# Splits of weights ordered behind copies of partial sums, and a shifted rotation of PSUM banks, in a two-layer decoder trunk

## The chip, the core and the metric

The kernel runs on one core of a Trainium2 chip. A core has five engines that work side by side, each through its own queue of instructions: PE (TensorE: matmuls, which write to the accumulator memory PSUM), DVE (VectorE), ACT (ScalarE), POOL (GpSimd) and SP (SyncE, which here only starts transfers). The metric is the device time of one execution in microseconds (us), lower is better; the median of several runs is given.

## The reference

The input is one sequence of 512 tokens with 1024 features. Two layers are run, each of three sub-layers that are added to `x`: half of a SwiGLU feed-forward (hidden width 2816), a mixer, half of a second feed-forward.

```python
def swiglu(h, w_gate, w_up, w_down):
    return (jax.nn.silu(h @ w_gate) * (h @ w_up)) @ w_down
...
    for l in range(DEPTH):
        x = x + 0.5 * swiglu(rms_norm(x, ffn1_norm[l]), ffn1_w_gate[l], ffn1_w_up[l], ffn1_w_down[l])
        h = rms_norm(x, mix_norm[l])
        a, g, q, k, v = jnp.split(h @ w_in[l], splits, axis=-1)
        conv_out = conv_module(a, g, conv_w[l], conv_b[l], conv_norm[l])
...
        x = x + jnp.concatenate([conv_out, diff_out], axis=-1) @ w_out[l]
        x = x + 0.5 * swiglu(rms_norm(x, ffn2_norm[l]), ffn2_w_gate[l], ffn2_w_up[l], ffn2_w_down[l])
```

`conv_module` is a gated causal depthwise convolution of 31 taps; `diff_out` is a differential attention with four heads (two softmax maps each, biased by distance). All is float32.

## The kernel before

**Exact products from parts.** A float32 operand is split into a high part (rounded to the matmul's own type) and a low part (the rest), and a product is made of three matmuls: high by high, high by low, low by high. `parts_of` (L98 on) splits a weight tile: ACT copies it to `whi` (L100), DVE, or POOL in the mixer, subtracts to get `wlo` (L101). The tiles come from rings: five slots for raw weights (`wraw`), four for sums of weights (`wsum`), nine each for `whi` and `wlo`. A split can run when its raw tile is there and a slot of the rings is free.

**The feed-forward.** The 22 hidden blocks of 128 are done in three parts: "first" (6 blocks, plain products), "seven" (8) and "last" (8). In the last two, products of two by two blocks are made with seven block products instead of eight. Gate and up weights of a hidden block make one *group*: from the four halves `g1`, `g2`, `u1`, `u2` (loaded by SP, and by POOL where a transfer adds to what is in the tile, L159) come the seven operands `u2u1`, `u2`, `g1`, `g2`, `all`, `g1u2u1`, `g1u1` (class `Sums`; `all` and `g1u2u1` are added on DVE, L174 and L175). `seven` (L390 on) runs a group: four accumulators `a`, `d` (one PSUM bank) and `b`, `c` (the other), 256 columns each; each `go` adds 12 matmuls (L407) to one of them. Between them ACT saves partial sums in `keep` (L412, L416, L421), because the accumulators go on to add the next product. The last product of a group (`rest`, with `g1u1`) runs inside the next group, through `before`. `Hidden.add` (L445 on) then splits the hidden block (ACT L456, DVE L457) and, at every second one, makes the sums of blocks (DVE L462 to L464, ACT L466, DVE L467); `big`, `sum` and `last` are handles to these.

**The down products** of a part run as four *pairs* of output blocks (`Pair`, L477 on, matmuls L496) in the same scheme, with their own groups of weights. `head` makes the first product into `c` and saves it (L503). For pair 0 `body` makes `a`, saves it (L513), makes most of `b` and `d`, runs the head of pair 1, then the rest, and saves `a` and `d` (L523). For the others it makes `d`, runs the finish of the pair before, makes `a`, saves both (L529), makes `b`, `c`, `a`, and saves `a` (L533).

**Banks.** `pair_banks` (L345) gives two PSUM banks of one of three tags, which rotate: sc, po, mm. Each tag has two banks, so a tag comes round at every third request. In the mixer fixed tags meet this rotation: `softmaxes` uses sc and po, `project_values` uses mm, the output projection sc and po. The mixer asks in this order: two pairs in `begin` for the convolution, one for `conv_in(2)`, two for the keys, two for the queries, one for `conv_in(3)`. `to_features` transposes queries (PE L818) in the bank of their product, and ACT copies them out (L825).

**What sets the order.** The program is traced as text; when it is built, a scheduler puts each engine's instructions in an order with the help of a simulated timeline, among instructions that are ready there, and adds the semaphores. Matmuls marked `keep_in_program_order` stay in the order of the text. `behind(i, ...)` adds to each instruction that is traced inside it and runs on the engine of `i` an edge that puts it after `i`; it is an order on that engine alone, so with a handle of ACT it holds the high parts (L100), with one of DVE the low parts (L101).

In the function `ffn`, `fetch` starts the loads of a group's sums, `group` the rest, and `weights` or `split` the splits. Only two places were ordered by `behind` in the pairs: the splits made for pair 0 behind `hid.big` and `hid.sum`, those of pair 1 behind `hid.last`.

Of the kernel before, what the change touches and what calls it, by code (L numbers as in the profile page):

```python
# [22 lines left out]
KT = DM // P  # L23
# [46 lines left out]
def trunk(ctx: ExitStack, tc: tile.TileContext, xt, par, lamv, relb, onehot,  # L70
# [271 lines left out]

    turns = iter(range(1000))

    def pair_banks():  # L345
        tag = ("sc", "po", "mm")[next(turns) % 3]
        return [bank(tag, "ps_pair") for _ in range(2)]


    class Halves:  # L350
# [32 lines left out]
        def get(self, name):  # L383
# [3 lines left out]
            k0, c = {"b11": (0, 0), "t1": (0, HS), "b21": (KT // 2, 0), "b22": (KT // 2, HS)}[name]  # L387
            return lambda j: (acth[:, k0 + j, c : c + HS], actl[:, k0 + j, c : c + HS])

    def seven(halves, w, banks, fp, before, last):  # L390

        a, d = banks[0][:, :HS], banks[0][:, HS:]
        b, c = banks[1][:, :HS], banks[1][:, HS:]
        two = banks[1].rearrange("p (n c) -> p n c", n=2)
        keep = fp.tile([P, 4, HS], F32, tag="gn", name="keep", bufs=2)
        g = keep[:, 0::2]

        def go(ps, wt, xt, first=False):  # L400


            at = halves.get(xt)
            for j in range(KT // 2):
                (wh, wl), (xh, xl) = wpart([w[wt]], j), at(j)
                for i, (l, r) in enumerate(((wh, xh), (wh, xl), (wl, xh))):
                    mm = T.matmul(ps, l, r, start=first and i == j == 0, stop=False, skip_group_check=True)  # L407
# [69 lines left out]
    class Pair:  # L477
# [25 lines left out]
            self.saved = S.activation(self.keep[:, self.kc], self.c, AF.Copy)  # L503
            return self

        def body(self, w, before):
            a, b, c, d, go = self.a, self.b, self.c, self.d, self.go
            both = self.banks[0].rearrange("p (n c) -> p n c", n=2)
            if self.m == 0:
                n = self.hid.n  # L510
                most, rest = range(n - 1), range(n - 1, n)
                go(a, w["g1"], "b11")
                S.activation(self.keep[:, 0], a, AF.Copy)  # L513
# [9 lines left out]
                S.activation(self.keep[:, 2:], both, AF.Copy)  # L523
            else:
                nxt = None
                go(d, w["u2"], "t4")
                before()
                go(a, w["g1"], "b11")
                S.activation(self.keep[:, :2], both, AF.Copy)  # L529
                go(b, w["g2"], "b21")  # L530
                go(c, w["all"], "b22")
                go(a, w["g1u2u1"], "t2")
                S.activation(self.keep[:, 2], a, AF.Copy)  # L533
# [17 lines left out]
    def ffn(fp, pr, gu, dn, after, begun, then, aside=None):  # L551
        halves = None
        late = []
        jobs = []
# [20 lines left out]
        for fs, kind in PARTS:  # L575
            many = len(fs)
            hh, held = [], []
            if kind == "first":
# [55 lines left out]
            pair = None  # L634
            for m in range(KT // 2):
                m2 = m + KT // 2
                if m == 0:
                    with behind(hid.big, hid.sum):
                        ahead[0].split("u2u1")
                        this.split("all", "g1u2u1", "g1u1")  # L640
                    pair = Pair(hid, fp, m, m2).head(this.w["u2u1"])
                    nxt = pair.body(this.w, lambda: Pair(hid, fp, 1, 1 + KT // 2).head(ahead[0].w["u2u1"]))
                else:
                    if m == 1:
                        with behind(*hid.last):
                            this = group()
                            this.weights()
                        pair = nxt
                    else:
                        this = group()  # L650
                        this.weights()
                        pair = Pair(hid, fp, m, m2).head(this.w["u2u1"])
                    pair.body(this.w, finish)
                if kind == "last":
                    if m:
# [366 lines left out]
    for l in range(DEPTH):  # L1022
# [12 lines left out]
        with tc.tile_pool(name="ffn", bufs=1) as fp:  # L1035
            begun = ffn(fp, pr, gu1[l], dn1[l], preparing("mix_norm"), begun,
                        lambda tail: begin(nxt["p"], [[wag[l, c, i] for i in range(2)] for c in range(2)], tail),
                        aside if l == 0 else None)
        mixer(l, nxt["p"], preparing("ffn2_norm"), begun)
        with tc.tile_pool(name="ffn", bufs=1) as fp:  # L1040
            begun = begin(nxt["p"], [[gu2[l, m, i] for i in range(2)] for m in range(2)])
            if l + 1 < DEPTH:
                begun = ffn(fp, nxt["p"], gu2[l], dn2[l], preparing("ffn1_norm", l + 1), begun,
                            lambda tail: begin(nxt["p"], [[gu1[l + 1, m, i] for i in range(2)] for m in range(2)], tail))
            else:
                ffn(fp, nxt["p"], gu2[l], dn2[l], store, begun, lambda tail: tail())
        pr = nxt["p"]


# [72 lines left out]
```

## Time and profile before

| | us |
|---|---|
| median of three runs | 1803.24 (1803.14 to 1806.4) |
| the profiled execution | 1801.71 |
| its span, first to last instruction | 1799.7 |
| granted TensorE clock, mean over the span | 0.997 |

| stretch of PE (start to end in the profiled execution) | from | to |
|---|---|---|
| first feed-forward of layer 0, up groups of "seven" | 108.4 | 189.2 |
| its pairs | 189.1 | 229.7 |
| up groups of "last" | 229.5 | 311.8 |
| its pairs | 311.6 | 353.6 |
| output projection of the mixer of layer 0 | 508.5 | 555.3 |
| output projection of the mixer of layer 1 | 1400.9 | 1450.0 |

In a group's row stand the engine, the line, the operation and the tiles written and read; then the number of instructions, their busy time, the mean duration of one in ns, and the idle time of the engine before them with what ended it. A row of waits reads: who waited, for whom, total us, times, longest. A row of the order in time reads: start, duration, engine, line, operation, tiles, shapes, and in brackets the idle time before it and what ended it. Times are from the start of the span. Rows of several alike instructions in a run are merged (x2, x8).

### The profile page before, as it was taken

The page shows a single profiled execution, that of the slowest core. Times are in us where ns is not written, and L with a number is a line of the kernel's source. Part 1 is how long each engine was busy: PE and PEld are TensorE (multiplying, and loading weights), DVE is VectorE, ACT ScalarE, POOL GpSimd, SP SyncE. Part 2 cuts the span into 40 slices and gives each one's busy share as a digit, 9 for nine tenths or more (in the row PEclk, how much of TensorE's full clock was granted, in tenths as well). Part 3 has the DMA queues.
Part 4 walks back from the last instruction along what each step waited for, and adds up shares of the span by engine and source line. Part 5 has one row for each costly group of instructions (what it writes and reads, how often), then busy time and mean ns, then how long its engine had stood idle before and what let it go on. Part 6 is the DMA issues. An engine that isn't in the chain of part 4 may idle for free.

```text
span 1799.7 us, 33063 instructions
## 1 busy us (share of the span) xinstructions
PE 1768.5 (98%) x11844; PEld 1622.7 (90%) x11844; DVE 1477.8 (82%) x2595; ACT 1034.1 (57%) x1930; POOL 554.6 (31%) x523
## 2 busy tenths in 40 slices
PE   8999999999999999999999999999999999999998
PEld 7799999988778899999988999999877888999998
DVE  7969888969867869889977788888688588698886
ACT  5546566655845446566644565666558454465664
POOL 3011212379942011112310111133897320112121
PEclk9999999999999999999999999999999999999999
DMA  6457777633212547777643677766231135577774
GB/s 219 133 139 184 176 185 173 153 101 105 60 48 88 140 119 181 170 190 177 152 126 108 154 185 177 184 160 168 78 99 48 48 106 132 127 186 176 180 179 123
DMA packets 163012, 253.57 MB, mean 141 GB/s; under 512 B 18871, under 2 KB 60614, under 8 KB 162848
## 3 DMA queue, kind: packets, MB, share of 16 engines
q1 hardware_dynamic: 126144, 197.19, 35.4%
q0 software_dynamic: 36416, 54.12, 18.8%
q8 instruction: 92, 1.51, 0.4%
q14 instruction: 72, 0.59, 0.1%
q10 hardware_dynamic: 288, 0.16, 0.0%
HBM read 249.28 MB, written 3.42 MB: 140 GB/s over the span
## 4 chain that ended last, share of the span: by engine, by line
PE 90%; ACT 4%; DVE 2%; issue 1%; DMA 1%; POOL 1%; SPq 0%; ACTq 0%; DVEq 0%; POOLq 0%
PE ps_pair L407 36%; PE ps_pair L496 14%; PE ps_pair L202 9%; PE ps_pair L199 9%; PE ps_pair L203 9%; PE ps_out L199 2%; PE ps_out L202 2%; PE ps_out L203 2%; PE ps_pair L781 2%; PE ps_pair L780 2%; PE ps_pair L779 2%; ACT whi L100 1%; PE ps_sc L896 1%; DVE wlo L101 1%; PE ps_v L809 1%
## 5 line engine op out<-in xcount | busy, mean ns | idle before, releaser
L100 ACT ACTIVATE whi<-wraw 128x512 fp32r<-128x512 f32 x736 | 448.8, 628 | 465.4 <-PE ps_pair L202 160.1
L101 DVE TENSOR_TENSOR wlo<-wraw,whi 128x512 fp32r<-128x512 f32 x648 | 445.1, 709 | 113.5 <-ACT whi L100 98.1
L159 POOL DMA_DIRECT2D wsum<-in_gu x128 | 112.2, 912 | 717.4 <-DMA wsum<-in_gu 302.0
L407 PE MATMUL ps_pair<-actl,whi 128*128 128x256 f32 x1024 | 290.2, 283 | 0.0
L407 PE MATMUL ps_pair<-acth,wlo 128*128 128x256 f32 x1024 | 290.2, 283 | 0.0
L407 PE MATMUL ps_pair<-acth,whi 128*128 128x256 f32 x1024 | 290.2, 283 | 0.0
L407 PE MATMUL ps_pair<-tl,whi 128*128 128x256 f32 x768 | 217.7, 283 | 0.0
L407 PE MATMUL ps_pair<-th,wlo 128*128 128x256 f32 x768 | 217.7, 283 | 0.0
L407 PE MATMUL ps_pair<-th,whi 128*128 128x256 f32 x768 | 217.7, 283 | 0.0
L199 PE MATMUL ps_pair<-acth,whi 128*128 128x512 f32 x512 | 200.8, 395 | 5.6 <-ACT whi L100 5.6
L202 PE MATMUL ps_pair<-actl,whi 128*128 128x512 f32 x512 | 200.2, 392 | 0.0
L203 PE MATMUL ps_pair<-acth,wlo 128*128 128x512 f32 x512 | 199.1, 391 | 0.0
L407 PEld LDWEIGHTS ps_pair<-acth,whi 128*128 128x128 f32 x1024 | 196.8, 192 | 0.2
L407 PEld LDWEIGHTS ps_pair<-actl,whi 128*128 128x128 f32 x1024 | 196.8, 192 | 0.2
L407 PEld LDWEIGHTS ps_pair<-acth,wlo 128*128 128x128 f32 x1024 | 196.8, 192 | 0.0
L159 POOL DMA_DIRECT2D wsum<-in_dn x112 | 99.0, 1191 | 266.0 <-DVE wlo L101 108.0
L101 DVE TENSOR_TENSOR wlo<-wsum,whi 128x512 fp32r<-128x512 f32 x192 | 131.7, 693 | 30.6 <-ACT whi L100 29.3
L407 PEld LDWEIGHTS ps_pair<-th,whi 128*128 128x128 f32 x768 | 147.6, 192 | 0.0
L407 PEld LDWEIGHTS ps_pair<-th,wlo 128*128 128x128 f32 x768 | 147.6, 192 | 0.0
L407 PEld LDWEIGHTS ps_pair<-tl,whi 128*128 128x128 f32 x768 | 147.6, 192 | 0.0
L100 ACT ACTIVATE whi<-wsum 128x512 fp32r<-128x512 f32 x192 | 118.8, 623 | 47.1 <-PE ps_pair L202 16.7
L496 PE MATMUL ps_pair<-hl,whi 128*128 128x256 f32 x512 | 145.1, 283 | 0.0
(201 smaller groups left out, 4498.7 us busy)
## 6 DMA issues: line engine op xcount, KB each, us to landing
wraw<-in_gu SPq DMA_DIRECT2D x288, 256.0 KB, 3.5
wsum<-in_gu SPq DMA_DIRECT2D x128, 256.0 KB, 3.8
wsum<-in_gu POOLq DMA_DIRECT2D x128, 256.0 KB, 4.9
wraw<-in_dn SPq DMA_DIRECT2D x68, 256.0 KB, 3.5
wraw<-in_wqkv SPq DMA_DIRECT2D x48, 256.0 KB, 2.8
wraw<-in_dn SPq DMA_DIRECT2D x64, 128.0 KB, 4.0
wraw<-in_wag SPq DMA_DIRECT2D x32, 256.0 KB, 3.0
wraw<-in_wout SPq DMA_DIRECT2D x32, 256.0 KB, 2.9
```

The lines of the kernel that those rows point to most:

```text
L100: S.activation(hi, raw, AF.Copy)
L101: (eng or V).tensor_tensor(out=lo, in0=raw, in1=f32(hi), op=ALU.subtract)
L159: nc.gpsimd.dma_start(dst[:, to], src, accum_op=ALU.add)
L199: first = T.matmul(ps, wh, xh, start=start, stop=False)
L202: T.matmul(ps, wh, xl, start=False, stop=False)
L203: T.matmul(ps, wl, xh, start=False, stop=stop)
L407: mm = T.matmul(ps, l, r, start=first and i == j == 0, stop=False, skip_group_check=True)
L496: mm = T.matmul(ps, s[:, f], r, start=side not in self.begun, stop=False, skip_group_check=True)
L779: T.matmul(ps[n], xh[:, t], wh, start=k == 0, stop=False)
L780: T.matmul(ps[n], xh[:, t], wl, start=False, stop=False)
L781: T.matmul(ps[n], xl[:, t], wh, start=False, stop=k == KT - 1)
L809: T.matmul(ps, xh[:, t], wh, start=k == 0, stop=False)
```

## The change

First, the splits of a group are traced inside `group` and stand behind a copy: `saves` collects the copies that end a group's or a pair's use of `keep` (L421, L523, L533), and a group's splits come behind the last but one of them at that point of the text, or behind what `after` names (for pair 1 `hid.last`, as before). For pair 0 the splits of `all`, `g1u2u1` and `g1u1` move out of the block behind `hid.big` and `hid.sum`: they are now traced inside `body`, behind the copy L513 and behind `hid.last[0]` (L466). Second, `skip` passes over turns of the bank rotation: in the first feed-forward of layer 0 one turn before the down products of "first" and one before the groups of "seven"; in its second feed-forward and in the first of layer 1 one before "seven"; none in the last.

```diff
+    def skip(n):
+        for _ in range(n):
+            next(turns)
...
+    saves = []
...
-        S.activation(keep[:, 2], a, AF.Copy)
+        saves.append(S.activation(keep[:, 2], a, AF.Copy))
...
-        def body(self, w, before):
+        def body(self, w, before, more=None):
...
-                S.activation(self.keep[:, 0], a, AF.Copy)
+                more(S.activation(self.keep[:, 0], a, AF.Copy))
...
-                S.activation(self.keep[:, 2:], both, AF.Copy)
+                saves.append(S.activation(self.keep[:, 2:], both, AF.Copy))
...
-                S.activation(self.keep[:, 2], a, AF.Copy)
+                saves.append(S.activation(self.keep[:, 2], a, AF.Copy))
...
-        def group():
-            ahead[0].loads()
+        def group(part=False, after=()):
+            this = ahead[0]
+            this.loads()
             fetch()
-            return ahead.pop(0)
+            ahead.pop(0)
+            with behind(*(after or saves[-2:-1])):
+                if part:
+                    this.split("u2u1", "g1", "g2")
+                    this.add()
+                    this.split("u2")
+                else:
+                    this.weights()
+            return this
...
+                skip(spare[0])
...
+            if kind == "seven":
+                skip(spare[1])
             for mm, m in enumerate(fs):
-                rest = seven(halves, group().weights(), pair_banks(), fp, finish, mm == many - 1)
+                rest = seven(halves, group().w, pair_banks(), fp, finish, mm == many - 1)
...
-            this = group()
-            this.split("u2u1", "g1", "g2")
-            this.add()
-            this.split("u2")
+            this = group(part=True)
...
                 if m == 0:
+
+                    def more(saved):
+                        with behind(saved, hid.last[0]):
+                            this.split("all", "g1u2u1", "g1u1")
+
                     with behind(hid.big, hid.sum):
                         ahead[0].split("u2u1")
-                        this.split("all", "g1u2u1", "g1u1")
                     pair = Pair(hid, fp, m, m2).head(this.w["u2u1"])
...
-                    if m == 1:
-                        with behind(*hid.last):
-                            this = group()
-                            this.weights()
-                        pair = nxt
-                    else:
-                        this = group()
-                        this.weights()
-                        pair = Pair(hid, fp, m, m2).head(this.w["u2u1"])
+                    this = group(after=hid.last if m == 1 else ())
+                    pair = nxt if m == 1 else Pair(hid, fp, m, m2).head(this.w["u2u1"])
```

More of the change, by code (lines that the diff above doesn't have):

```diff
@@ L549, in begin, with ffn @@
         return [*zip(ws, ps)], first_products(pr, ws, ps, early=tail is not None, tail=tail)
-    def ffn(fp, pr, gu, dn, after, begun, then, aside=None):
+    def ffn(fp, pr, gu, dn, after, begun, then, spare, aside=None):
         halves = None
@@ L637, in ffn @@
                 if m == 0:
+                    def more(saved):
+                        with behind(saved, hid.last[0]):
+                            this.split("all", "g1u2u1", "g1u1")
                     with behind(hid.big, hid.sum):
                         ahead[0].split("u2u1")
-                        this.split("all", "g1u2u1", "g1u1")
                     pair = Pair(hid, fp, m, m2).head(this.w["u2u1"])
-                    nxt = pair.body(this.w, lambda: Pair(hid, fp, 1, 1 + KT // 2).head(ahead[0].w["u2u1"]))
+                    nxt = pair.body(this.w, lambda: Pair(hid, fp, 1, 1 + KT // 2).head(ahead[0].w["u2u1"]), more)
                 else:
-                    if m == 1:
-                        with behind(*hid.last):
-                            this = group()
-                            this.weights()
-                        pair = nxt
-                    else:
-                        this = group()
-                        this.weights()
-                        pair = Pair(hid, fp, m, m2).head(this.w["u2u1"])
+                    this = group(after=hid.last if m == 1 else ())
+                    pair = nxt if m == 1 else Pair(hid, fp, m, m2).head(this.w["u2u1"])
                     pair.body(this.w, finish)
@@ L1037, in trunk @@
                         lambda tail: begin(nxt["p"], [[wag[l, c, i] for i in range(2)] for c in range(2)], tail),
-                        aside if l == 0 else None)
+                        (l == 0, 1), aside if l == 0 else None)
         mixer(l, nxt["p"], preparing("ffn2_norm"), begun)
@@ L1043, in trunk @@
                 begun = ffn(fp, nxt["p"], gu2[l], dn2[l], preparing("ffn1_norm", l + 1), begun,
-                            lambda tail: begin(nxt["p"], [[gu1[l + 1, m, i] for i in range(2)] for m in range(2)], tail))
+                            lambda tail: begin(nxt["p"], [[gu1[l + 1, m, i] for i in range(2)] for m in range(2)], tail), (0, 1))
             else:
-                ffn(fp, nxt["p"], gu2[l], dn2[l], store, begun, lambda tail: tail())
+                ffn(fp, nxt["p"], gu2[l], dn2[l], store, begun, lambda tail: tail(), (0, 0))
         pr = nxt["p"]
```

## The prediction

> **What bounds the kernel now.** I read the page first, then TensorE's waits, then the order of work on each engine around the longest of them.
>
> ```profile
> PE 1768.5 (98%) x11844; PEld 1622.7 (90%) x11844; DVE 1477.8 (82%) x2595; ACT 1034.1 (57%) x1930; POOL 554.6 (31%) x523
> L407 PE MATMUL ps_pair<-actl,whi 128*128 128x256 f32 x1024 | 290.2, 283 | 0.0
> PE ps_pair L496 <- ACT keep L513: 6.8, 8, 0.8
> PE ps_pair L496 <- ACT keep L533: 3.1, 4, 1.2
> PE ps_pair L496 <- ACT keep L523: 1.7, 8, 0.2
> PE ps_out L199 <- ACT acth L880: 1.4, 2, 1.2
> PE ps_v L809 <- DVE gl L751: 0.8, 1, 0.8
> ```
>
> PE sets the end: it is busy for 98% of the span, and the up-product groups (L407) never wait. What can be won lies in a few waits. Eight equal ones (two in each feed-forward: one per part) end with the copy L513, eight with L523, four with L533; the rest shown is in the mixers. So 11.6 us (6.8 + 3.1 + 1.7) are waits of PE for copies on ACT. The first of the eight L513 waits:
>
> ```profile
> 192.78 0.28 PE L496 MATMUL ps_pair<-hl,whi 128*128 128x256 f32 x1
> 192.90 0.28 PE L496 MATMUL ps_pair<-hh,wlo 128*128 128x256 f32 x1
> 194.02 0.39 PE L496 MATMUL ps_pair<-yh,whi 128*128 128x256 f32 x1 [0.84 <-ACT keep L513]
> 194.25 0.28 PE L496 MATMUL ps_pair<-yl,whi 128*128 128x256 f32 x1
> 190.70 0.38 ACT L503 ACTIVATE keep<-ps_pair 128x256 f32<-128x256 f32 x1 [1.48 <-PE ps_pair L496]
> 191.53 0.61 ACT L100 ACTIVATE whi<-wsum 128x512 fp32r<-128x512 f32 x1
> 192.05 1.14 ACT L100 ACTIVATE whi<-wraw 128x512 fp32r<-128x512 f32 x2
> 193.09 0.61 ACT L100 ACTIVATE whi<-wsum 128x512 fp32r<-128x512 f32 x1
> 193.61 0.36 ACT L513 ACTIVATE keep<-ps_pair 128x256 f32<-128x256 f32 x1
> 193.88 0.83 ACT L466 ACTIVATE yh<-ht 128x768 fp32r<-128x768 f32 x1
> ```
>
> PE computes `a` (12 matmuls), nine of `b`, then wants `d`, which shares `a`'s bank and so waits until L513 has read `a`. Matmuls follow each other at 0.12 us here, so `a` is complete nine matmuls and one drain before 192.90 + 0.12: its last starts at 191.82 and ends at 192.10. The copy runs only at 193.61, because ACT, which had no idle time between, is making four high parts: one for the next pair, then `all`, `g1u2u1`, `g1u1` of this one.
>
> **Part 1: three splits go behind L513 and L466.** New order on ACT: 191.53 the next pair's high part, L513 at 192.14 (its `a` is there), done 192.50; `d` may start at 193.02 without a wait. The gap goes from 1.12 us start to start to 0.12, and the slow second start (194.02 to 194.25, 0.23) goes too: 1.11 us, times 8 = **8.9 us**. What is late next is `all`:
>
> ```profile
> 191.79 0.42 DVE L464 SCALAR_TENSOR_TENSOR ht<-ht,hid 128x256 f32<-128x256 f32 x1
> 192.73 0.68 DVE L101 TENSOR_TENSOR wlo<-wsum,whi 128x512 fp32r<-128x512 f32 x1
> 195.14 0.95 DVE L467 TENSOR_TENSOR yl<-ht,yh 128x768 fp32r<-128x768 f32 x1
> 198.53 0.69 DVE L175 TENSOR_TENSOR wraw<-wraw 128x512 f32<-128x512 f32 x1
> ```
>
> L466 needs L464 (done at 192.21), so it follows L513: 192.50 to 193.33; the high part of `all` is there at 193.9. DVE does the next pair's low part until 193.4, L467 until 194.35, the low part of `all` until 195.0. PE does nine of `d` (1.08) and the next pair's head (1.44), wants `all` at 195.54 and its low part two matmuls later, at 195.8. The margin is 0.8 us; `g1u2u1` and `g1u1` follow 0.6 apart and are used later. Behind them on ACT stand three splits of the next pair: by the same count the low part of its `u2` ends at 196.9, and PE wants it 51 matmuls after 193.02, at 199.1. The raw slots of the three splits come free some 1.5 us later, and so do the loads that SP and POOL issue into them; these are for the pair two further on, about 10 us ahead of their use, and cost nothing while that holds. Bounds: 8.9, and 0 if a new wait takes all of it.
>
> **Part 2: each group's high parts behind the copy two groups earlier.** In the up groups L407 has no idle to win. Nine slots hold seven parts a group, so `u2` takes the slot that `g1u1` of two groups before gives back 36 matmuls into the group between: 60 matmuls (7.2 us) ahead of its use, for a split of 0.6 and a subtraction of 0.7. A copy of 0.36 ahead of that costs nothing; without the cover it would be 0.36 a group. In the pairs it moves L523 ahead of the split of pair 2, and L533 of pair 1 ahead of those of pair 3:
>
> ```profile
> 199.32 1.16 ACT L100 ACTIVATE whi<-wraw 128x512 fp32r<-128x512 f32 x2 [2.04 <-DVE wraw L175]
> 200.38 1.13 ACT L100 ACTIVATE whi<-wsum 128x512 fp32r<-128x512 f32 x2
> 201.42 0.57 ACT L523 ACTIVATE keep<-ps_pair 128x512 f32<-128x512 f32 x1
> 335.03 0.63 ACT L100 ACTIVATE whi<-wsum 128x512 fp32r<-128x512 f32 x1 [1.59 <-PE ps_pair L496]
> 335.57 0.36 ACT L533 ACTIVATE keep<-ps_pair 128x256 f32<-128x256 f32 x1
> 334.63 0.28 PE L496 MATMUL ps_pair<-yh,wlo 128*128 128x256 f32 x1
> 335.99 0.39 PE L496 MATMUL ps_pair<-yh,whi 128*128 128x256 f32 x1 [1.08 <-ACT keep L533]
> ```
>
> At 335.57 L533 has stood behind a split that itself waited 1.59 us. Its `a` was ready 24 matmuls (2.9 us) before 334.63 + 0.12. Put ahead, it can start when ACT's last work before that idle time ends (335.03 - 1.59 = 333.4) and is done by 333.8, and the stall goes: 335.99 - 334.63 - 0.12 = 1.24, and 0.11 for the second start, 1.35 us. The same pair of layer 1 has the longest such wait, 1.2, so 1.45. Together **2.8 us**, bounds 0 and 2.8. The other two L533 waits (3.1 - 1.1 - 1.2 = 0.8) are of pairs 2 and 3, and no split that stands ahead of those copies is moved; they stay.
>
> L523: 0.2 us of waiting, about as much of restart as above (0.27) make 0.48 a place, 3.8 in all. One of the four splits ahead of it goes behind it (0.52), but PE now comes 1.1 us sooner, while `all` of pair 1 still hangs on L175 (198.53), since DVE has no idle time before it. L523 is ready 51 matmuls after 193.02, at about 199.3, and that split at 199.32. If the copy comes first, 3.8 is won. If it waits for three splits it ends at 201.5, PE wants it 12 matmuls after 199.1, at 200.6: 0.9 + 0.1 lost instead of 0.48, so -4.2 in all. I take half of the better end, **1.9**, since the text has this copy ahead of those splits; bounds -4.2 and 3.8.
>
> **Part 3: the skipped turns.** The pairs of banks rotate sc, po, mm. Counted out, the last three of the mixer are sc, po, mm in layer 0 (queries, queries, conv) and po, mm, sc in layer 1; after the change mm, sc, po in both. The values (bank mm) then need only the first queries' copies.
>
> ```profile
> 445.85 0.39 PE L203 MATMUL ps_pair<-acth,wlo 128*128 128x512 f32 x1
> 1336.35 0.39 PE L202 MATMUL ps_pair<-actl,whi 128*128 128x512 f32 x1
> 1336.57 0.39 PE L203 MATMUL ps_pair<-acth,wlo 128*128 128x512 f32 x1
> 1339.09 1.43 PE L818 MATMUL ps_pair<-ident,qn 128*128 128x128 f32 x8 [2.13 <-DVE qn L794]
> 1341.08 0.80 PE L809 MATMUL ps_v<-whi,acth 128*128 128x512 f32 x1 [0.55 <-ACT qz L825]
> 1339.00:1341.00 2.00, 1.43 (x8) 0.88 (x8) 2.00 (x4) 1.24 (x3) 2.00 (x3) 0.74 0.34 123
> 1341.00:1347.00 6.00, 5.92 (x14) 4.67 (x15) 5.59 (x8) 3.96 (x7) 5.84 (x6) 0.52 0.31 89
> L203 PE MATMUL ps_out<-acth,wlo x96: 282/284/398, 509.9 to 555.0; 128*128 128x256 f32 x64, 128*128 128x512 f32 x32
> L203 PE MATMUL ps_out<-acth,wlo x96: 278/284/398, 1402.2 to 1449.7; 128*128 128x256 f32 x64, 128*128 128x512 f32 x32
> ```
>
> (The two rows of stretches end with the granted clock, the share of the DMA engines and GB/s.) In layer 1 PE idles 2.13 and 0.55 us, since the values' bank waits for the second queries, and these for L794. Its clock is granted at 0.52 in the next six: 14 matmuls in 5.92 us, 0.42 apart and not 0.22. From the last conv matmul to the last of the output projection layer 1 takes 1449.7 - 1336.57 = 113.1 us, layer 0, whose values only waited 0.8 for L751, 555.0 - 445.85 = 109.2. With the same banks I let layer 1 become like layer 0: **4.0 us**. Bounds 0 (the attention, on DVE and ACT, sets its own pace) and 6.5 (2.13 + 0.55 + 14 x 0.2, and 1 for slower transposes and restarts). Layer 0's 0.8 us I take as 0, bounds 0 and 0.9: its projection starts after a wait of 1.2 for the convolution (L880) anyway.
>
> [...]
>
> A skipped turn lets the next two pairs reuse banks after two turns instead of three. The tightest place is layer 0's first down product:
>
> ```profile
> 76.64 0.69 DVE L597 TENSOR_TENSOR gs<-ps_pair,rb 128x512 f32<-128x512 f32 x1
> 75.79 0.39 PE L199 MATMUL ps_pair<-hh,whi 128*128 128x512 f32 x1
> ```
>
> The bank read last at 77.3 is wanted 36 matmuls of 0.23 after 75.79, at 84: 6.7 us of cover, cost 0 (bounds 0 and 1).
>
> **Sum.** 8.9 + 2.8 + 1.9 + 4.0 = 17.6; I take back 1.0 for PE reaching later waits sooner (the L533 wait of 0.36 in pair 2 can grow). The profiled execution took 1801.71 us (span 1799.7), so 1785.1; the median of the runs lies 1.53 above it: **1786.6**. With the bounds of L523 and of part 3 this case runs from 1780 (8.9 + 2.8 + 3.8 + 7.4) to 1797 (8.9 + 2.8 - 4.2 - 1.0).
>
> **Rivals.** *The splits come too late* (slower). All three now stand behind L466, which needs DVE's L464. If the build's schedule puts L464 later than 192.21, `all` comes late: the first 0.8 us are free, each further one costs 8 us. From 2.9 us on ((2.9 - 0.8) x 8 = 16.8) nothing of the gain is left; at 4 us it is 25.6 - 16.6, so 1812. For it: DVE is full from 188 to 199. Against it: L464 stands ahead of every split there.
>
> *Only the banks help.* If the eight L513 gaps come from too few `whi` buffers and not from the order, they stay, and L523 and L533 too: 1803.2 - 4.0 = 1799.2. Against it: ACT never waited between 190.70 and 193.88; it worked. [...]
>
> *The clock falls all the same* in layer 1 with the wait gone: 14 x 0.2 = 2.8 stay, 1789.4.
>
> *No effect:* the edges ask for an order that the schedule loses elsewhere, and PE stays at its pace: 1803.
>
> **Chances.** Forecast 0.65, clock 0.06, banks only 0.08 (half of it under the line), no effect 0.06, splits late 0.15. A measurement of this kernel can tell about 0.2%, 3.6 us, from no change. Faster 0.65 + 0.06 + 0.04 = 0.75, same 0.04 + 0.06 = 0.10, slower 0.15. The range 1780 to 1804 leaves out the late splits.
>
> **What would show it.** Right: the row of PE waiting for L513 is gone, L513 starts within 0.3 us of the end of its `a`; no L533 wait above 0.5; in both mixers L809 follows L203 with no gap, and the clock stays at 1.00 in layer 1; L407 still without idle. Wrong: a new PE wait for L100 or L101 in the pairs, L523 waits of 0.8, or a mixer in layer 1 that still takes 113.

## The result, and the profile after

| | before | after |
|---|---|---|
| median of six runs, us | 1804.55 (1803.14 to 1806.46) | 1793.20 (1791.26 to 1793.69) |
| the profiled execution, us | 1801.71 | 1792.68 |
| its span, us | 1799.7 | 1790.9 |
| granted TensorE clock, mean | 0.997 | 0.995 |

The changed kernel takes 0.9935 of the time before, 95% interval 0.9922 to 0.9947: 11.4 us less in the medians, 8.8 in the spans of the two profiled executions. 1786.6 was forecast, so the sign and the range were right, and of the forecast gain of 16.6 about two thirds came.

The new text shifts the lines: the pair matmuls L496 are now L502, the copies L503, L513, L523, L529, L533 are L509, L519, L529, L535, L539, L466 is L472, the values L809 are L821, the transposes L818 are L830, L880 is L892. **The name L529 thus changes its meaning**: before, it was the copy of `a` and `d` in the middle of pairs 1 to 3; that copy is L535 now. Kernels below that are made from the kernel before, or have lines added, differ from these by a few; where it matters the text says so.

TensorE's waits after, the columns being total, times and longest:

```profile
PE ps_pair L502 <- ACT keep L535: 2.8, 5, 0.9
...
PE ps_out L199 <- ACT acth L892: 2.2, 2, 1.7
PE ps_pair L502 <- ACT keep L539: 0.5, 1, 0.5
```

The three rows of pair waits of before (6.8, 3.1 and 1.7 us) have become one of 0.5 and a new one of 2.8, for a copy that nobody waited for. The output projection waits for the convolution (L892), 2.2 in place of 1.4. By stages (start of the first to end of the last matmul in the order of PE's work; a mixer counts from the end of its last conv matmul):

| stage | before | after |
|---|---|---|
| the eight stretches of pairs, sum | 330.9 | 319.6 |
| mixer of layer 0, last conv matmul to last of the output projection | 109.0 | 112.4 |
| mixer of layer 1, the same | 113.0 | 111.6 |

So the pairs give 11.3, the two mixers together take 2.0, and the rest of the span takes 0.5.

**The pairs.** ACT's order around the first of the eight places, and PE where it waited before:

```profile
191.64 0.62 ACT L100 ACTIVATE whi<-wsum 128x512 fp32r<-128x512 f32 x1
192.25 0.38 ACT L519 ACTIVATE keep<-ps_pair 128x256 f32<-128x256 f32 x1
192.53 0.84 ACT L472 ACTIVATE yh<-ht 128x768 fp32r<-128x768 f32 x1
...
199.45 0.60 ACT L529 ACTIVATE keep<-ps_pair 128x512 f32<-128x512 f32 x1 [2.69 <-PE ps_pair L502]
199.95 0.62 ACT L100 ACTIVATE whi<-wraw 128x512 fp32r<-128x512 f32 x1
```

```profile
193.01 0.28 PE L502 MATMUL ps_pair<-hh,wlo 128*128 128x256 f32 x1
193.13 0.28 PE L502 MATMUL ps_pair<-yh,whi 128*128 128x256 f32 x1
```

One split, the copy of `a`, L472, and only then the other splits: the copy starts when `a` is there, and `d` (193.13) follows `b` at the usual 0.12 us. At 199.45 the copy that closes pair 0 (once L523) runs ahead of the split of `all` of pair 1 at 199.95, the tie that the forecast left open.

What was not foreseen, in the part "last", pair 2:

```profile
332.57 1.15 ACT L100 ACTIVATE whi<-wraw 128x512 fp32r<-128x512 f32 x2 [1.63 <-DVE wraw L175]
...
335.19 0.71 ACT L291 ACTIVATE acth<-x,par 128x512 fp32r<-128x512 f32 x1
335.80 0.62 ACT L299 ACTIVATE sq<-x 128x512 f32<-128x512 f32 x1
336.32 1.14 ACT L100 ACTIVATE whi<-wraw 128x512 fp32r<-128x512 f32 x2
337.36 0.58 ACT L535 ACTIVATE keep<-ps_pair 128x512 f32<-128x512 f32 x1
```

```profile
337.37 0.28 PE L502 MATMUL ps_pair<-hh,wlo 128*128 128x256 f32 x1
338.00 0.39 PE L502 MATMUL ps_pair<-yh,whi 128*128 128x256 f32 x1 [0.34 <-ACT keep L535]
```

ACT sits idle for 1.63 us because the split at the head of its queue needs a sum that DVE has not made (L175). Then seven splits (three of them left out here) and the next stage's preparation (L291, L299) follow without a gap, and the copy stands behind them.

**The mixers.** The values start without a gap in both, as forecast. The loss stands ahead of the output projection; stretches of PE's time, with busy time and count by engine, then granted clock, share of DMA, GB/s:

```profile
501.00:506.00 5.00, 1.75 (x9) 1.08 (x9) 3.74 (x11) 2.44 (x7) 4.65 (x5) 0.89 0.01 3
506.00:512.00 6.00, 5.78 (x15) 4.68 (x16) 5.25 (x8) 4.11 (x9) 3.26 (x4) 0.52 0.00 0
1389.00:1394.00 5.00, 2.58 (x11) 1.58 (x11) 3.78 (x11) 2.72 (x8) 4.61 (x5) 0.83 0.00 0
1394.00:1400.00 6.00, 5.74 (x15) 4.54 (x16) 5.57 (x9) 3.97 (x7) 3.06 (x4) 0.57 0.00 0
```

The same stretches of layer 0 before:

```profile
503.00:508.00 5.00, 3.27 (x21) 2.32 (x19) 4.68 (x21) 4.34 (x18) 4.22 (x4) 1.00 0.02 3
508.00:514.00 6.00, 5.50 (x29) 4.57 (x30) 4.31 (x10) 4.04 (x8) 2.82 (x3) 1.00 0.00 0
```

Before, PE was busy for 3.27 of the 5 us ahead of the projection, and its clock held at 1.00; after, for 1.75, and the next six have a mean clock of 0.52: 15 matmuls are counted there, 29 before (some of them shorter). In layer 0 those of 512 columns start 0.43 us apart from 508.95 to 511.51, and 0.23 from 513.44 on. Summed over the matmuls that start late, this is some 2.5 us in each layer, an estimate from these two distances.

### The profile page after: what moved, and what is told of

Read it like the earlier page. It is cut to its first block, busy times and chain, and to the rows that moved or that the text cites. A ratio compares the mean times of both kernels' runs of the same rounds, so it can differ in the third digit from the quotient of the medians.

```text
span 1790.9 us, 32884 instructions
## 1 busy us (share of the span) xinstructions
PE 1767.7 (99%) x11844; PEld 1623.8 (91%) x11844; DVE 1475.3 (82%) x2595; ACT 1028.0 (57%) x1930; POOL 555.0 (31%) x523
## 4 chain that ended last, share of the span: by engine, by line
PE 90%; DVE 4%; ACT 4%; DMA 1%; issue 1%; POOL 1%; SPq 0%; ACTq 0%; DVEq 0%; POOLq 0%
PE ps_pair L413 36%; PE ps_pair L502 14%; PE ps_pair L202 9%; PE ps_pair L199 9%; PE ps_pair L203 9%; PE ps_out L199 2%; PE ps_out L202 2%; PE ps_out L203 2%; PE ps_pair L793 2%; PE ps_pair L792 2%; PE ps_pair L791 2%; ACT whi L100 1%; DMA wraw<-in_dn 1%; PE ps_v L821 0%; PE ps_sc L908 0%
## 5 line engine op out<-in xcount | busy, mean ns | idle before, releaser
L100 ACT ACTIVATE whi<-wraw 128x512 fp32r<-128x512 f32 x736 | 447.2, 627 | 419.0 <-PE ps_pair L202 163.1
L101 DVE TENSOR_TENSOR wlo<-wraw,whi 128x512 fp32r<-128x512 f32 x648 | 440.1, 698 | 108.8 <-ACT whi L100 93.5
L101 DVE TENSOR_TENSOR wlo<-wsum,whi 128x512 fp32r<-128x512 f32 x192 | 130.4, 685 | 20.2 <-ACT whi L100 16.3
L502 PE MATMUL ps_pair<-hh,whi 128*128 128x256 f32 x512 | 144.9, 283 | 0.0
L502 PE MATMUL ps_pair<-hl,whi 128*128 128x256 f32 x512 | 144.9, 283 | 0.0
```

The lines of the kernel that those rows point to most:

```text
L100: S.activation(hi, raw, AF.Copy)
L101: (eng or V).tensor_tensor(out=lo, in0=raw, in1=f32(hi), op=ALU.subtract)
L502: mm = T.matmul(ps, s[:, f], r, start=side not in self.begun, stop=False, skip_group_check=True)
```

## The experiments

The theory after these profiles: the edges carry all of the gain, the skipped turns give layer 1 its stall back and lose as much or more to a falling clock, and the L535 waits come from the splits that the edges moved. All times are medians with the ratio to the kernel before, measured beside it on the same chip. Sums over pairs and the two mixers are those of the profiled executions.

| kernel | median | ratio (95%) | pairs, sum | mixers |
|---|---|---|---|---|
| order_only | 1790.34 | 0.9918 (0.9904 to 0.9931) | 319.6 | 110.6, 111.2 |
| banks_only | 1804.00 | 0.9999 (0.9990 to 1.0008) | 332.3 | 110.6, 110.6 |
| three_only | 1790.53 | 0.9920 (0.9908 to 0.9933) | 318.7 | 109.0, 111.2 |
| saves_only | 1794.44 | 0.9942 (0.9929 to 0.9954) | 324.0 | 109.1, 111.9 |
| warm | 1787.09 | 0.9911 (0.9897 to 0.9924) | 317.5 | 109.8, 109.7 |
| mid_edge | 1792.86 | 0.9946 (0.9932 to 0.9959) | 319.9 | 111.2, 110.2 |
| mid_warm | 1788.96 | 0.9919 (0.9905 to 0.9932) | 320.1 | 109.0, 109.0 |
| mid_three | 1789.27 | 0.9920 (0.9907 to 0.9934) | 319.9 | 108.3, 108.6 |
| mid2_warm | 1788.61 | 0.9913 (0.9900 to 0.9927) | 317.3 | 109.0, 109.0 |
| mid2_three | 1784.82 | 0.9898 (0.9884 to 0.9911) | 315.9 | 108.1, 108.0 |
| mid2_banks | 1792.74 | 0.9941 (0.9929 to 0.9953) | 317.3 | 110.9, 111.2 |
| late | 1807.53 | 1.0022 (1.0012 to 1.0031) | 332.0 | 111.4, 110.4 |

### Each part alone

**order_only**: the changed kernel with no turn skipped.

```diff
-                        (l == 0, 1), aside if l == 0 else None)
+                        (0, 0), aside if l == 0 else None)
...
-                            lambda tail: begin(nxt["p"], [[gu1[l + 1, m, i] for i in range(2)] for m in range(2)], tail), (0, 1))
+                            lambda tail: begin(nxt["p"], [[gu1[l + 1, m, i] for i in range(2)] for m in range(2)], tail), (0, 0))
```

> The changed kernel without the skipped turns, so the edges alone. Theory (the edges carry the whole gain, the banks cost about 2 us): feed-forwards as in the changed kernel (10.7 us shorter than before), mixers as before, 109 us in layer 0 and 113 in layer 1, so about 1791 to 1792, 1 to 2 us below the changed kernel. Rival (the banks help by 4 us as forecast, and the edges are what lengthened the mixer of layer 0): mixer of layer 0 still 112, layer 1 115 or more, about 1797.

**banks_only**: the kernel before, with `skip` and `spare` as in the change and nothing else of it.

> The kernel before with the skipped turns alone. Theory: feed-forwards as before, the L513 waits all there (6.8 us), mixers 112.4 and 111.6 us as in the changed kernel with the clock of the output projection below 0.7 in its first 6 us, so about 1806, 2 us slower than before. Rival (banks help): layer 0 109, layer 1 109, about 1800.5.

**three_only**: of order_only the three splits of pair 0 alone.

```diff
-            with behind(*(after or saves[-2:-1])):
+            with behind(*after):
```

> Only the splits of all, g1u2u1 and g1u1 of pair 0 go behind the copy and the sums; no edge behind saves, no skipped turn. Theory: the L513 waits are gone (8.9 us), L523 wins its 3.8 or not by the tie of copy and split, L533 of pair 1 stays at 1.1 to 1.2, and no wait for the mid copy (L535) above 0.4 arises; mixers as before: 1792 to 1796. Rival (the saves carry the gain): above 1800.

**saves_only**: of order_only the edges behind `saves` alone; the three splits go back behind `hid.big` and `hid.sum`.

```diff
-                    def more(saved):
-                        with behind(saved, hid.last[0]):
-                            this.split("all", "g1u2u1", "g1u1")
...
                     with behind(hid.big, hid.sum):
                         ahead[0].split("u2u1")
+                        this.split("all", "g1u2u1", "g1u1")
```

> Only the edges behind saves; the three splits stay where they were, no skipped turn. Theory: L513 waits stay (6.8), L533 of pair 1 goes (2.8 won), the new L535 waits of pairs 2 and 3 come (about 3 to 5 lost): 1803 to 1806, no gain. Rival (the L535 waits come from PE being earlier after part 1 and not from these edges): no L535 wait above 0.4, 1800 to 1802.

Waits of PE in the pairs, first of three_only, then of saves_only:

```profile
PE ps_pair L502 <- ACT keep L535: 2.3, 4, 0.8
PE ps_pair L502 <- ACT keep L539: 1.2, 2, 0.7
```

```profile
PE ps_pair L502 <- ACT keep L519: 6.8, 8, 0.8
PE ps_pair L502 <- ACT keep L539: 0.5, 1, 0.5
PE ps_pair L502 <- ACT keep L535: 0.2, 1, 0.2
```

*The edges carry the gain*: order_only is 14 us faster than before, the turns alone measure as nothing. But within the edges the parts overlap. The three splits alone give 14 us (pairs 330.9 to 318.7). The `saves` edges alone give 10 (6.9 in the pairs), where the theory had no gain: they win pair 1's L533 and the L523 waits too. Both together give no more than the first alone. three_only has neither an L529 wait nor pair 1's L533 wait of 1.1 to 1.2: with the three splits out of the way the later copies come in time by themselves. (Its two L539 waits are those of the finish of pair 3, in the last feed-forward.)

The L535 wait had the wrong cause in the theory. saves_only hardly has it (0.2), three_only has it at 2.3: it comes with PE being earlier, not with the edges behind `saves`. Here the rival was right.

*The banks*: the theory had them 2 us slower alone, the rival 4 faster; neither came. Layer 1 went from 113.0 to 110.6, layer 0 from 109.0 to 110.6, and in both the clock falls at the projection (layer 0, five us before it and its first six; layer 1 has 2.63 busy and 0.72 too):

```profile
503.00:508.00 5.00, 2.63 (x14) 1.74 (x13) 4.29 (x15) 2.97 (x11) 3.84 (x5) 1.00 0.01 3
508.90:514.90 6.00, 5.86 (x21) 4.76 (x22) 5.69 (x9) 3.85 (x7) 2.95 (x4) 0.72 0.00 0
```

### Is it the clock?

**warm**: 14 spare matmuls behind the first three value products of the last block; they write columns that the fourth overwrites.

```diff
+WARM = (3, 4, 7)
...
                 if h < HEADS - 1:
+                    for _ in range(WARM[h] if i == 0 else 0):
+                        T.matmul(pos[i][:, 3 * VD :], ats[i, h][:, :P], vv[:, 0, h, :], start=True, stop=True)
                     return
```

> The changed kernel with 14 spare matmuls (each 128x128 f32, results overwritten) put into the pauses of PE in the last 6 us ahead of the output projection of each mixer. Theory (the clock falls because of those pauses, and that is what the changed mixers lose): granted clock 0.95 or more in the first 6 us of the output projection, which takes 46.8 us and not 48.3 to 48.8; mixers about 110 and 109; 4 to 5 us less than the changed kernel, about 1788.5. Rival (the convolution and attention end late, the clock only goes with it): the output projection starts later by what it gains, 1793.

The stretches ahead of the output projection and into it, in layer 0 (layer 1 has 5.32 busy and 1.00 too):

```profile
501.00:507.00 6.00, 5.32 (x40) 4.49 (x39) 4.54 (x12) 3.42 (x10) 5.45 (x6) 1.00 0.01 3
507.00:513.00 6.00, 6.00 (x31) 4.96 (x30) 5.34 (x9) 4.55 (x8) 2.85 (x3) 1.00 0.00 0
```

With PE kept busy for 5.32 of six us the clock stays at 1.00. The output projection, 48.8 and 48.3 us in the changed kernel, takes 46.3 in both layers, the mixers 109.8 and 109.7 instead of 112.4 and 111.6, and the median falls by 6.1, where 4 to 5 were expected. Of that the mixers give 4.5. Another 2.1 stand in the pairs (319.6 to 317.5; three L535 waits of 1.6 us in all, where there were five of 2.8), which the edit does not touch: they are not the clock, which is recorded as 1.00 in the changed kernel's pairs and has a mean of 1.000 over warm's span, and why they came stays open. The rival is ruled out: the projection starts as far behind the last conv matmul as before the edit (63.5 us in layer 0 of both kernels, 63.4 against 63.3 in layer 1). Work that computes nothing made the mixers faster, since it filled time in which PE waited anyway.

### The wait that took the place of the old ones

**mid_edge**: the changed kernel, with the splits of pairs 2 and 3 behind the copy L535 of the pair before.

```diff
-                S.activation(self.keep[:, :2], both, AF.Copy)
+                self.mid = S.activation(self.keep[:, :2], both, AF.Copy)
...
-                    this = group(after=hid.last if m == 1 else ())
+                    this = group(after=hid.last if m == 1 else (pair.mid,))
```

> The changed kernel, and the splits of pairs 2 and 3 stand behind the copy of a and d (L535) of the pair before. Theory (the new L535 waits, 4.0 us start to start in five places, come from splits that stand ahead of the copy on ACT): no L535 wait above 0.2, about 3 to 4 us less than the changed kernel, 1789 to 1790. Rival 1 (the copy is late because a and d are ready late, or because of ACT's other work there, L291 and L299): the waits stay, 1793. Rival 2 (the splits then come too late): new waits for L100 or L101 at the heads of pairs 2 and 3, slower than the changed kernel.

**mid_warm**: this and the spare matmuls. **mid_three**: three_only with the edge of mid_edge.

> The changed kernel with both edits of mid_edge and warm. Theory: the two gains add, since they lie in different stages: 7 to 9 us below the changed kernel, 1784 to 1786. Rival: one of them only, 1789.

> The three splits behind the copy and the sums, and the edge of mid_edge; no edge behind saves, no skipped turn. Theory: pairs as in mid_edge, that is 3 to 4 us below the kernel with the three splits alone (1790.5), mixers as before the change (109 and 111 to 113): about 1787. Rival (without the edges behind saves, pair 1's L533 waits come back once PE is earlier): 1789 to 1791.

ACT's order of mid_edge, around pair 2's copy and then pair 3's, and PE's waits:

```profile
336.31 0.57 ACT L535 ACTIVATE keep<-ps_pair 128x512 f32<-128x512 f32 x1
...
345.00 1.16 ACT L100 ACTIVATE whi<-wraw 128x512 fp32r<-128x512 f32 x2 [3.40 <-DVE wraw L175]
...
347.71 0.62 ACT L299 ACTIVATE sq<-x 128x512 f32<-128x512 f32 x1
348.23 0.62 ACT L100 ACTIVATE whi<-wraw 128x512 fp32r<-128x512 f32 x1
348.75 0.58 ACT L535 ACTIVATE keep<-ps_pair 128x512 f32<-128x512 f32 x1
```

```profile
PE ps_pair L502 <- ACT keep L535: 3.2, 3, 1.1
PE ps_pair L502 <- DVE wlo L101: 0.4, 1, 0.4
```

The edge did what it says: pair 2's copy runs at 336.31 and has no splits of pair 3 ahead of it. The wait only moved on, to pair 3's copy, and grew from 2.8 to 3.2 us. There too ACT had been idle for 3.4 us behind one split that waits for DVE's sum, with everything else queued behind it. The edge also has a price behind the pairs: the next stage's products behind the last finish start 4.6 us after the pairs and not 4.0, 1.8 us at three places. mid_edge gained nothing over the changed kernel, and its span equals that kernel's only because its mixers lost 2.6 us less (221.4 to 224.0). So mid_warm has one gain and not two, and is not better than warm.

mid_three, expected at 1787, is no better than three_only, and not for the rival's reason: no wait of pair 1 for L539 came back. Its pairs take 319.9, not 3 to 4 us less than 318.7, and it too pays the 1.8 behind them; its mixers, 216.9 in sum against 220.2, make up for that.

**mid2_warm** and **mid2_three**: mid_warm and mid_three, and the splits of the next stage's first weights behind pair 3's copy.

```diff
-        with behind(pair.saved):
+        with behind(pair.mid):
             return then(tail)
```

> mid_warm, and the splits of the next stage's first weights stand behind pair 3's copy of a and d (L535 there) instead of behind the copy after its head. Theory (in mid_edge and mid_warm the wait only moved on, from pair 2's copy to pair 3's, since the next stage's splits then stood ahead of that one): the three waits of 1.07 at 349, 892 and 1236 go (1.23 start to start each), nothing takes their place, about 3.5 us below mid_warm (1789.0): 1785 to 1786, and 1.5 below warm (1787.1). Rival (ACT is late there because DVE makes the sums L175 late, 3.4 us of ACT's idle time ahead of the split): the waits stay or move on again, 1788 to 1790.

> mid_three with the same edit: no edge behind saves, no skipped turn, no spare matmuls. Theory: the same 3.5 us, 1785 to 1786 from 1789.3. Rival: 1788 to 1790, as above.

No wait for L535 is listed in either. Yet the pairs of mid2_warm, 317.3, stand level with those of warm, 317.5, and the next stage's products behind the last finish now start 4.7 to 4.8 us after the pairs (350.2 to 355.0 in mid2_three), where it was 4.0 (350.1 to 354.1 in the changed kernel): some 0.7 at three places, 2 us given back. mid2_three met its number: against mid_three its pairs give 4.0 (319.9 to 315.9) and the later starts take 0.5 of that, the 3.5 that was expected. Against three_only the pairs give 2.8, of which the later starts take back 2, and the mixers 4.1 (220.2 to 216.1). mid2_warm missed its expectation and is not told apart from mid_warm. Its pairs give 2.8 against mid_warm's and the later starts take 0.5, but its profiled execution spends 2.3 more ahead of the first pairs (191.5 against 189.2); whether that is the kernel or the execution stays open.

That gain in the mixers was not expected; mid_three already has 3.3 of it, and the same order on DVE as mid2_three. DVE's order at the last of the queries, in layer 1 of the kernel before (three_only has the same order), and in layer 0 of mid2_three (layer 1 has the same):

```profile
1337.00 0.69 DVE L751 TENSOR_TENSOR gl<-ps_pair,rb 128x512 f32<-128x512 f32 x1 [1.60 <-PE ps_pair L203]
1337.60 0.75 DVE L865 SCALAR_TENSOR_TENSOR ps_y<-u,par,ps_y 128x512 f32<-128x512 f32 x1
1338.26 1.28 DVE L794 TENSOR_TENSOR qn<-ps_pair,rs_y 128x512 f32<-128x512 f32 x2
```

```profile
442.19 1.28 DVE L806 TENSOR_TENSOR qn<-ps_pair,rs_y 128x512 f32<-128x512 f32 x2
443.60 0.69 DVE L763 TENSOR_TENSOR gl<-ps_pair,rb 128x512 f32<-128x512 f32 x1
```

Before, DVE stands idle for 1.60 us at the gate of the last convolution product, with the queries' normalization queued behind it. There PE's wait of 2.13 us for `qn` (L794) came from; the forecast let the banks take it away by keeping the values off that wait. In mid2_three the normalization is ahead, the wait is gone with no turn skipped, and of layer 1's stall 0.9 is left. No edge of the two kernels names these instructions; that the schedule took this order there is a side effect, and what in it tipped the order stays open.

### The turns on a better order

**mid2_banks**: mid2_three with the skipped turns of the change.

> mid2_three with the skipped turns of the change, the cleanest look at what the turns are worth: everything else is the same text. Theory (values start at once, attention ends ahead of the convolution, PE pauses and its clock falls ahead of the output projection): mixers 110 to 112 us instead of 108.1 and 108.0, values from +-0.2 us of the last conv matmul, clock below 0.9 in the first 6 us of the output projection, 4 to 6 us above mid2_three (1784.8): 1789 to 1791. Rival (the turns win what the values wait for there, 0.8 and 1.8 us, and the clock stays): 1782 to 1784.

The clearest run on the banks, and the wrong way round for them: 7.9 us slower than mid2_three in the medians, mixers 222.1 instead of 216.1. PE's order behind the last conv matmul, in mid2_three and in mid2_banks:

```profile
443.40 1.03 PE L830 MATMUL ps_pair<-ident,qn 128*128 128x128 f32 x8
444.34 0.50 PE L821 MATMUL ps_v<-whi,acth 128*128 128x512 f32 x1
449.47 2.74 PE L908 MATMUL ps_sc<-kt,qz 128*128 128x512 f32 x6
```

```profile
443.92 0.39 PE L821 MATMUL ps_v<-whi,acth 128*128 128x512 f32 x1
449.37 1.03 PE L830 MATMUL ps_pair<-ident,qn 128*128 128x128 f32 x8
455.70 2.74 PE L908 MATMUL ps_sc<-kt,qz 128*128 128x512 f32 x6
```

`qn` is ready at the same point in both. Where the bank is free at once, the schedule runs the values first; the transposes, which lead to the scores and to the whole softmax on DVE, come 5.5 us later, counted from the end of the last conv matmul (443.6 and 444.1), the scores 5.7 later, and the output projection starts 62.7 us after that point instead of 60.1. The clock falls as well; first six us of the projection in layer 0, of mid2_banks (layer 1 has 0.61 too) and of mid2_three (1.00 too):

```profile
506.80:512.80 6.00, 6.00 (x17) 4.71 (x18) 5.74 (x9) 3.71 (x6) 2.81 (x4) 0.61 0.00 0
```

```profile
503.00:509.00 6.00, 5.13 (x25) 3.51 (x24) 5.57 (x14) 3.56 (x9) 3.92 (x4) 1.00 0.00 0
```

How much is which can be read against mid2_warm, which has the skipped turns too, and besides the edges behind `saves` and the spare matmuls, with which its clock holds (a mean of 0.999 over its span, where mid2_banks has 0.996): its projection starts as late, 62.7 us behind the last conv matmul, and its mixers take 109.0. So of the 2.8 and 3.2 us that a mixer of mid2_banks takes longer than one of mid2_three, some 0.9 and 1.0 come from the later attention and 1.9 and 2.2 from the clock. (The start is 2.6 later and costs less than that, since mid2_three's projection takes 48.0 us at full clock and mid2_warm's 46.3.)

The short wait that the turns remove held the values back just long enough for more urgent work.

### How large are the margins?

**late**: the changed kernel, with the three splits behind L535 in pairs 1 to 3 as well (`more` is defined for every pair; there it puts them behind the copy alone).

```diff
-                S.activation(self.keep[:, :2], both, AF.Copy)
+                more(S.activation(self.keep[:, :2], both, AF.Copy))
...
-                    this = group(after=hid.last if m == 1 else ())
+                    this = group(part=True, after=hid.last if m == 1 else ())
```

> The changed kernel, and in pairs 1 to 3 too the three splits of all, g1u2u1 and g1u1 stand behind that pair's own copy of a and d (L535), as those of pair 0 stand behind L513. It tests the arithmetic of margins by which the splits of pair 0 were held to be in time: behind the copy stand only 12 matmuls of b (1.44 us) and two of c, 1.68 us in all, but a drain of 0.28, the copy 0.57, the high part 0.52 and the low part 0.68 make 2.05. Theory: no L535 wait is left (2.8 us of waits, 4.0 start to start won), but PE waits about 0.4 for the low part of all (L101) in each of the 24 pairs, 9 us: 1797 to 1799. Rival (the margin is larger than counted, since DVE or ACT take these splits first): no wait for L101, 1789.

```profile
PE ps_pair L502 <- DVE wlo L101: 7.2, 25, 0.7
PE ps_pair L413 <- ACT keep L418: 1.7, 2, 1.0
PE ps_pair L502 <- DVE hl L463: 1.5, 4, 0.4
```

Each of the 24 pairs waits for its low part, mostly 0.38 to 0.39 from start to start beyond the usual 0.12, as the count from rows had it (0.4), and no wait for L535 is left. Other waits came that the count did not have, in pair 0 (L463, once L457, the low part of a hidden block) and in the up groups (L418, once L412, a copy into `keep`), so the median is 14 us above the changed kernel and not 4 to 6. So an edge of the same kind turns the gain into a loss where the margin is negative: pair 0 had most of `b`, most of `d` and the next pair's head to cover the splits, a later pair only `b`.

## Why the prediction was right, and where not

- **L513, 8.9**: right in size and in place. All eight waits are gone; the copy starts 0.04 us after its `a` ends (last start 191.93 + 0.28). The margin of 0.8 held: no wait for L100 or L101 in the pairs, so the rival of late splits fell; late shows that its arithmetic was sound.
- **L523, 1.9 taken of -4.2 to 3.8**: it came out at the upper end, 8 x 0.48 = 3.8; the tie went to the copy. three_only wins it without the edge that the forecast gave as its reason.
- **L533 of pair 1, 2.8**: won; together with a third wait of 0.36, which the forecast left standing. Here too either part alone does it, so the terms of parts 1 and 2 were no sum of separate causes, though their total came close.
- **The 1.0 taken back for later waits**: mis-sized. Five L535 waits, with the second starts and three small ones 5.1 us from start to start, stand in its place. Its mechanism, PE reaching later waits sooner, is what three_only showed against saves_only, but the wait named (pair 2's L533) was not the one that grew. Pairs and the rest of the feed-forwards: 12.6 forecast (8.9 + 2.8 + 1.9 - 1.0), 10.8 found (8.8 + the 2.0 of the mixers).
- **The banks, 4.0**: this step failed. "With the same banks I let layer 1 become like layer 0" is true of the two layers after, which follow one schedule; false is that this schedule is layer 0's of before. Both layers change, to 112.4 and 111.6. In layer 1 the stall went and the clock during the values stayed at 1.00, as forecast. The clock then fell ahead of the projection, which no term held. Counted by warm's mixers, where it does not fall (1.000 over each of warm's four runs), layer 1 won 3.3 of the 4.0 and lost 1.9 of that to the clock; layer 0 lost 2.5 to the clock and 0.8 more, whose cause stays open. The lower bound of 0 for layer 1 named the right reason, that the attention sets its own pace, and layer 0's bounds of 0 to 0.9 left out a loss.
- **The rival "the clock falls all the same"** named the falling clock, in the wrong place: behind the values, in layer 1 only. It falls 60 us later, in both, at 504.88 and at 1392.34. "Only the banks help" and "no effect" are ruled out by order_only and banks_only.

Of the 7.8 us between the 16.6 forecast and the 8.8 of the profile, 6 are the banks (+4.0 against -2.0) and 1.8 the feed-forwards. The signs listed ahead were right on the first step, the second and the values; that the clock stays at 1.00 in layer 1 held behind the values and failed at the projection, for which they listed nothing.

## What to carry to other kernels

ACT stood idle here for 1.63 and 3.40 us with other work queued behind an instruction that waited for data, and the copies L535 among that work came late: TensorE waited 2.8 us for them in the changed kernel and 3.2 in mid_edge. So ask which instruction at the head of an engine's queue waits, and what small copies for TensorE are queued behind it. When a wait is removed, look for the next copy on the same queue and at what the freed engine will now do first; a wait can be what lets urgent work pass, as in mid2_banks, where the queries' transposes came 5.5 us later with the values' wait gone. Look also at TensorE's pauses ahead of a dense stage: here they came with a mean clock of 0.52 and 0.57 in the projection's first six us, and 14 matmuls that compute nothing, with which the clock stayed at 1.00, took the mixers from 112.4 and 111.6 us to 109.8 and 109.7. The best kernel here, mid2_three, 18.9 us faster than before in the medians, needed neither them nor the skipped turns.

## What was not expected of the hardware

The clock fell here after pauses shorter than the 2.13 us of layer 1 before. In the changed kernel's layer 0 the last five are 0.53, 0.79, 0.37, 0.78 and 1.75 us with work between; the recorded clock falls at 504.88, 0.41 us into the last of them, and the mean clock from 506 to 512 is 0.52. The waits do not decide it alone. order_only and three_only list the same ones of TensorE in the mixers' last part (1.6 us in five for L931 ahead of L938, 0.8 in two for L953, 1.2 in one for L892); the first six us of the projection of layer 0 from 506, in the one and in the other:

```profile
506.00:512.00 6.00, 5.24 (x18) 4.12 (x19) 4.25 (x11) 3.29 (x7) 3.08 (x3) 0.72 0.00 0
```

```profile
506.00:512.00 6.00, 5.56 (x29) 4.63 (x30) 4.31 (x10) 4.04 (x8) 2.76 (x3) 1.00 0.00 0
```

The mixer of layer 0 took 110.6 us in the one and 109.0 in the other. Nor does the kernel alone decide it: of the five runs of order_only the slowest, of 1792.49 us, has a mean clock of 0.997 and the fastest, of 1788.82, one of 1.000. So a mixer's row in the table can differ by some 1.6 us for the clock alone, an estimate from the 110.6 and 109.0.

In the traces of the kernel before and of the changed kernel the recorded clock is 1.00 or 0.50 and nothing between; 0.52 and 0.57 are means over six us that lie mostly in a stretch of 0.50. (At 0.50, matmuls of 512 columns follow each other at 0.43 us in the changed kernel's projection, at 1.00 at 0.23.) Ahead of the program's end these two traces have three stretches of 0.50, each 6.83 us long: from 1339.97 before, from 504.88 and 1392.34 after. The stretches of 1.00 around them, 1331.20 and 450.56 us before, 494.93, 880.64 and 389.12 after, are 390, 132, 145, 258 and 114 times 3.4133 us, half of 6.83. In the 3.41 us ahead of each of the three falls PE was busy for 1.28, 1.75 and 1.57 us. What tipped it between the executions of order_only and three_only was not shown.

At the output projection the first six us have a mean clock of 0.52 and 0.57 in the two mixers of the changed kernel, 0.72 in both of banks_only and 0.61 in both of mid2_banks, which all have skipped turns and no spare matmuls. Without skipped turns it is 0.72 in layer 0 of order_only, and 1.00 in layer 0 of the kernel before, in layer 0 of three_only and in both layers of mid2_three. In layer 1 of the kernel before the clock fell at the values instead: 0.52 from 1341 to 1347.
